# The start of a two-block transformer kernel: modulation weights become the stationary operand, the x/rms products change engine, and a fourth FFN chunk joins the tile-by-tile work

## The chip, the cores and the metric

The kernel runs on one core of one Trainium2 chip. The metric is device time in microseconds (us) of one execution. Engines are called by the short names of the profile: PE is TensorE (matmuls), PEld its weight loads, DVE is VectorE, ACT is ScalarE, POOL is GpSimd, SP issues most of the DMAs. L820 is line 820 of the kernel.

## The reference, cut to what matters

Two blocks run one after the other on x (512 tokens, width 1024). The part that the change touches is the very start of the first block: the modulation vectors and the first FFN's input.

```python
mod = (jax.nn.silu(c) @ ada_w + ada_b).reshape(b, 9, D_MODEL)          # c: 1024 values
mod_ctx = (jax.nn.silu(c_ctx) @ ada_w + ada_b).reshape(1, 9, D_MODEL)  # the same weights, a second vector
...
h = modulate(rms_norm(x, norm_pre), mod[:, 0], mod[:, 1])   # h * (1 + scale) + shift
y = (silu(h @ w_gate) * (h @ w_up)) @ w_down                # d_ff = 2816
x = x + 0.5 * mod[:, 2] * rms_norm(y, norm_post)
```

Everything after it (the context stream, the mixer, the second FFN, two attention blocks) is the same in both kernels.

## The kernel before

All of x and every hidden state lie transposed in SBUF: eight tiles k = 0..7 of 128 features by 512 tokens. A product in the precision that is wanted is made of three fp32r matmuls: each operand is split into a high part (a cast on ACT, L77 or L99) and a low part (a subtraction on DVE, L78 or L100), and high by high, high by low and low by high are added in PSUM. A weight chunk of 128 by 1024 (512 KB) is loaded by SP into `raw` (`eraw` during the start, a ring of six buffers) and split by `wchunk`.

The start (`start`, everything ahead of L1529) works as follows. SP loads x, then sixteen half chunks of `ada_w`, with FFN chunks of `f1_gu` in between. `start_squares` and `start_norm` (L1539 to L1563) make 1/rms and the eight products x/rms, called `xr`; these products run on POOL. Eight modulation chunks are made by `ada_chunk` (L230): chunk j = 4m + q gives quarter q (two of the eight feature tiles) of modulation row m, and rows 0 (shift) and 1 (scale) are needed at once. The chunks come in pairs, (q, 4+q), for q = 0..3. Each is two half chunks, each split as above, and 16 matmuls in which the stationary operand is the four columns of `c4` (two condition vectors, high and low parts) and the moving operand is 256 columns of weights (L237). That leaves a result of 4 rows by 256 columns in PSUM; ACT copies it out (L240, tile `asb`), and two small fp32 matmuls with the constant `comb` (L244) transpose it and add high and low parts; DVE adds the bias into `mod` (L247).

When pair q is there, DVE makes the scales `s1` of tiles 2q and 2q+1 (L1518), ACT makes the modulated tile `st` (L1522) and its high part `hhx` (L99), DVE its low part `hlx` (L100). Then the FFN chunks loaded so far are multiplied by these two tiles (`mm_run`, L820: 3 matmuls per tile and chunk, each 128x128 by 128x512). Three FFN chunks are worked tile by tile in this way (gate and up of f = 0, gate of f = 1), in buffers lent by tiles that are needed later (`ya`, `yc`); their sums lie in PSUM banks `y` and `pt`. The fourth (up of f = 1) is an ordinary chunk of `ffn`, multiplied by L96 in one run of 24 matmuls, and so are all that follow. PSUM has eight banks under four names; in the start x sums and norms use `pt` and `y`, modulation uses `px` and `s`.

A scheduler with priorities orders each engine's instructions; each engine then runs its own list strictly in that order. After the start, the other 28 modulation chunks are made piece by piece on DVE (`ada_sums`), five pieces per weight chunk after the first seven calls of `wchunk` in the FFN.

Of the kernel before, what the change touches and what calls it, by code (L numbers as in the profile page):

```python
# [7 lines left out]
F32 = mybir.dt.float32  # L8
F32R = mybir.dt.float32r
# [3 lines left out]
ALU = mybir.AluOpType  # L13
# [6 lines left out]
KT = D // 128  # L20
# [3 lines left out]
SLOT = 1024  # L24
# [12 lines left out]
class K:  # L37
# [135 lines left out]
    def norm_steps(self, x, y, c, G, h, s, shift, xd, run):  # L173

        r = {}

        def put():
            for k in range(KT):
                self.nc.sync.dma_start(xd[k][:, c], x[k][:, c])

        out = [lambda: r.update(p=self.rstd(y, c, run))]
        out += [lambda k=k: self.post_norm_add(x, y, c, G, r["p"], range(k, k + 2)) for k in range(0, KT, 2)]
        out += [lambda: r.update(n=self.rstd(x, c, run))]
        out += [lambda k=k: self.norm_split(x, c, h, s, shift, r["n"], range(k, k + 2)) for k in range(0, KT, 2)]
        return out + [put]
# [28 lines left out]
    def ada_setup(self):  # L214
        nc, c = self.nc, self.const
        cc = c.tile([128, KT, 2], F32, name="cc")
        nc.sync.dma_start(cc, self.I["cc"])
        sc = self.sc = c.tile([128, KT, 2], F32, name="sc")
        nc.scalar.activation(sc, cc, AF.Silu)
        self.c4 = c.tile([128, KT, 4], F32R, name="c4")  # L220
        nc.scalar.copy(self.c4[:, :, 0:2], sc)
        nc.vector.tensor_tensor(self.c4[:, :, 2:4], sc, self.c4.bitcast(F32)[:, :, 0:2], op=ALU.subtract)
        self.comb = c.tile([4, 2], F32, name="comb")
        nc.scalar.dma_start(self.comb, self.I["comb"])
        self.mod = c.tile([128, 9, KT, 2], F32, name="mod")

    def ada_chunk(self, j):

        nc = self.nc
        m, q = divmod(j, 4)  # L230
        t = self.ps("a")
        ps = t[0:4, 0:256]
        for a in range(2):
            w = self.wchunk(self.I["ada_w"][j, a])
            for i in range(2):
                for k in range(4):
                    nc.tensor.matmul(ps, self.c4[:, 4 * a + k, :], w[i][:, k * 256:(k + 1) * 256],  # L237
                                     start=(a == 0 and i == 0 and k == 0), stop=(a == 1 and i == 1 and k == 3))
        sb = self.ap.tile([4, 256], F32, name="asb", tag="asb", bufs=2)
        nc.scalar.copy(sb, ps)  # L240

        def end():
            for u in range(2):
                nc.tensor.matmul(t[:, 256 + 2 * u:258 + 2 * u], sb[:, u * 128:(u + 1) * 128], self.comb,  # L244
                                 start=True, stop=True)
            b = self.v("ada_b")[:, m * KT + 2 * q:m * KT + 2 * q + 2]
            nc.vector.tensor_tensor(self.mod[:, m, 2 * q:2 * q + 2, :],  # L247
                                    t[:, 256:260].rearrange("p (a b) -> p a b", b=2),
                                    b.unsqueeze(2).to_broadcast([128, 2, 2]), op=ALU.add)

        return end

    def ada_sums(self, j):

# [1092 lines left out]
    def run(self):  # L1347
        tc, nc, I = self.tc, self.nc, self.I
        H = (slice(0, 256), slice(256, 512))
        with ExitStack() as es:  # L1350
            self.setup(es)
            self.banks("x:pt y/m:pt y/a:px s")
            h = self.hl(es.enter_context(tc.tile_pool(name="hp", bufs=1)), T, "x")
# [6 lines left out]
            yp = rh.enter_context(tc.tile_pool(name="yp", bufs=1, side="right"))  # L1360
            ra = ExitStack()
            xa = ra.enter_context(tc.tile_pool(name="xa", bufs=1, side="right"))
            x = self.tiles(xa, T, "xa")
            with tc.tile_pool(name="st", bufs=1) as self.ap:
                with tc.high_priority(offset=AHEAD):
                    self.ada_setup()
                    first = self.start(self.ap, x, h, [(xa, "ya", 4), (xa, "ya", 4), (yp, "yc", 2)])
            self.banks("x:px s pt/m:y/a:y")
            y = [xa.tile([128, 2, T], F32, name="ya", tag="ya", bufs=4) for _ in range(4)]
            y = [t[:, j, :] for t in y for j in range(2)]  # L1370
            yc = [yp.tile([128, 4, TC], F32, name="yc", tag="yc", bufs=2) for _ in range(2)]
            yc = [t[:, j, :] for t in yc for j in range(4)]
# [29 lines left out]
            with tc.tile_pool(name="ssa", bufs=1) as sp:  # L1402
                with tc.tile_pool(name="fop", bufs=1) as fp, tc.tile_pool(name="csp", bufs=1) as gp:
# [11 lines left out]
                    f = self.fourier(fw, h, fp)  # L1415
# [11 lines left out]
            x, y = self.tiles(xb, T, "xb"), self.tiles(xb, T, "yb")  # L1427
# [34 lines left out]
            for l in range(2):  # L1462
# [4 lines left out]
                with tc.tile_pool(name="at", bufs=1) as self.at:  # L1467
                    mm = self.attention(l, h)
                    x = [mg.tile([128, 4, T], F32, name=q, tag=q) for q in ("yth", "ytl")]
                    x = [t[:, j, :] for t in x for j in range(4)]  # L1470
# [21 lines left out]
    def start(self, pool, x, h, rooms):  # L1492


        nc = self.nc
        for k in range(KT):
            nc.sync.dma_start(x[k], self.I["xT"][k])
        nc.sync.dma_start(self.tri, self.I["tri"])
        nc.sync.dma_start(self.vec, self.I["vec"])
        self.early = pool  # L1500
        self.s1 = [self.const.tile([128, KT], F32, name=f"s1{w}") for w in range(2)]
        sq = self.start_squares(pool, x)
        ends = [[self.ada_chunk(q), self.ada_chunk(4 + q)] for q in range(2)]
        self.start_norm(pool, x, sq)
        out, ws = [], []

        def chunk(i):
            p, tag, bufs = rooms[i]
            into = [p.tile([128, SLOT], F32R, name=tag, tag=tag, bufs=bufs) for _ in range(2)]
            ws.append(self.wchunk(self.I["f1_gu"][i // 2, i % 2], into=into))  # L1510
            out.append(self.ps("x"))

        for q in range(4):
            for f in ends[q]:
                f()
            ks = slice(2 * q, 2 * q + 2)
            for w in range(2):
                nc.vector.scalar_tensor_tensor(self.s1[w][:, ks], self.mod[:, 1, ks, w], 1.0, self.v("f1pre")[:, ks],  # L1518
                                               op0=ALU.add, op1=ALU.mult)
            for k in (2 * q, 2 * q + 1):  # L1520
                t = pool.tile([128, T], F32, name="st", tag="st", bufs=2)
                nc.scalar.activation(t, self.xr[k], AF.Identity, bias=self.mod[:, 0, k, 0:1], scale=self.s1[0][:, k:k + 1])  # L1522
                self.split(h[k][0], h[k][1], t)
            if q < 2:
                for i in range(2 * q, min(2 * q + 2, len(rooms))):
                    chunk(i)
                ends.append([self.ada_chunk(q + 2), self.ada_chunk(q + 6)])
            done = [range(0, 2 * q + 2) if q == 1 and i > 1 else range(2 * q, 2 * q + 2) for i in range(len(ws))]
            for w, t, kk in zip(ws, out, done):  # L1529
                self.mm_run(t, w, h, slice(0, T), kk)  # L1530
        self.early = None
        return list(zip(ws, out))
# [12 lines left out]
    def start_norm(self, pool, x, acc):  # L1545

        nc = self.nc
        ps = self.ps("m")
        for j in range(4):
            nc.tensor.matmul(ps[:, j:j + 1], acc[:, j * 128:(j + 1) * 128], self.ones[:, 0:1], start=True, stop=True)  # L1550
        v = pool.tile([128, 4], F32, name="sv")
        nc.vector.tensor_scalar(v, ps[:, 0:4], 1.0 / D, EPS, op0=ALU.mult, op1=ALU.add)
        rt = self.rsqrt(pool, v, [128, 4], "s")
        r = self.ps("m")
        for j in range(4):
            nc.tensor.matmul(r[:, j * 128:(j + 1) * 128], rt[:, j:j + 1].to_broadcast([128, 128]), self.ident,
                             start=True, stop=True)
        rs = pool.tile([128, T], F32, name="srs")
        nc.vector.tensor_copy(rs, r)
        self.xr = []  # L1560
        for k in range(KT):
            self.xr.append(pool.tile([128, T], F32, name=f"xr{k}"))
            nc.gpsimd.tensor_tensor(self.xr[k], x[k], rs, op=ALU.mult)  # L1563

    def ctx_norm(self, pool, hc):

# [109 lines left out]
def lay_out(i):  # L1676

    def fm(a):
        return np.ascontiguousarray(a.T.reshape(KT, 128, -1))

    o = {"xT": fm(i["x"][0]), "cT": fm(i["ctx"][0])}
    o["cc"] = np.ascontiguousarray(np.stack([i["c"][0].reshape(KT, 128).T, i["c_ctx"].reshape(KT, 128).T], axis=2))
    o["comb"] = np.array([[1, 0], [0, 1], [1, 0], [0, 1]], np.float32)
    items = [("ada_b", i["ada_b"][0])]
    for p, n in (("f1", "ffn1"), ("mx", "mix"), ("f2", "ffn2")):
        items += [(p + "pre", i[n + "_norm_pre"][0]), (p + "post", i[n + "_norm_post"][0])]
# [10 lines left out]
    w = i["w_in"][0]  # L1697
# [12 lines left out]
    w = i["w_in_2"]  # L1710
# [40 lines left out]
```

## Time and profile before

| | |
|---|---|
| time, median of 3 runs | 3499.43 us (3496.61 to 3499.68) |
| profiled execution: own time | 3494.87 us |
| profiled execution: span from first to last instruction | 3493.1 us |
| mean granted TensorE clock | 0.991 |
| HBM traffic over the span | 94 GB/s |

The span is what the profile describes; the time of an execution is a little longer (here 1.8 us). Busy shares are per engine over the span. A matmul's row lasts longer than the spacing to the next one, since matmuls are pipelined; rates are read from start to start. One instruction in fp32r leaves one record of PE and one of PEld; one in plain fp32 leaves two of each (the four-fold sums of L1550 and L1556, four instructions each, stand in the trace with x8).

### The profile page before, as it was taken

The page shows a single profiled execution, that of the slowest core. Times are in us where ns is not written, and L with a number is a line of the kernel's source. Part 1 is how long each engine was busy: PE and PEld are TensorE (multiplying, and loading weights), DVE is VectorE, ACT ScalarE, POOL GpSimd, SP SyncE. Part 2 cuts the span into 40 slices and gives each one's busy share as a digit, 9 for nine tenths or more (in the row PEclk, how much of TensorE's full clock was granted, in tenths as well). Part 3 has the DMA queues.
Part 4 walks back from the last instruction along what each step waited for, and adds up shares of the span by engine and source line. Part 5 has one row for each costly group of instructions (what it writes and reads, how often), then busy time and mean ns, then how long its engine had stood idle before and what let it go on. Part 6 is the DMA issues. An engine that isn't in the chain of part 4 may idle for free.

```text
span 3493.1 us, 49244 instructions
## 1 busy us (share of the span) xinstructions
PE 3428.1 (98%) x19332; PEld 2937.4 (84%) x19332; DVE 2011.8 (58%) x4119; ACT 1288.2 (37%) x2334; POOL 103.1 (3%) x147
## 2 busy tenths in 40 slices
PE   7999999999899999999999999999999999999998
PEld 5888889878888887888889898889788888898888
DVE  7466554857742338835545664556935454656545
ACT  5312212546533224424432343433434342334332
POOL 1000000002100000000100000000000100000000
PEclk9999999999899999999999999999999999999999
DMA  5344442422223334132432322233223423233231
GB/s 200 97 132 122 137 146 69 137 77 67 74 90 97 102 95 124 64 105 71 124 100 86 118 93 92 96 115 95 100 73 88 135 82 107 79 108 104 97 109 55
DMA packets 120720, 354.65 MB, mean 102 GB/s; under 512 B 17304, under 2 KB 28184, under 8 KB 120232
## 3 DMA queue, kind: packets, MB, share of 16 engines
q1 hardware_dynamic: 108976, 333.93, 29.6%
q0 software_dynamic: 7360, 12.59, 1.5%
q10 hardware_dynamic: 4152, 4.98, 0.4%
q8 instruction: 152, 2.49, 0.3%
q14 instruction: 80, 0.66, 0.1%
HBM read 320.47 MB, written 8.42 MB: 94 GB/s over the span
## 4 chain that ended last, share of the span: by engine, by line
PE 91%; DVE 5%; issue 2%; DMA 1%; ACT 1%; POOL 1%; SPq 0%; DVEq 0%; ACTq 0%; POOLq 0%
PE px L96 36%; PE s L96 17%; PE pt L96 15%; PE y L922 3%; PE s L463 2%; PE px L463 1%; PE px L794 1%; PE px L795 1%; PE pt L915 1%; PE px L798 1%; PE pt L463 1%; PE pt L820 1%; DVE wlo L78 1%; PE px L820 1%; PE s L820 1%
## 5 line engine op out<-in xcount | busy, mean ns | idle before, releaser
L78 DVE TENSOR_TENSOR wlo<-raw,whi 128x1024 fp32r<-128x1024 f32 (+4 forms) x549 | 587.0, 1075 | 614.4 <-ACT whi L77 290.0
L77 ACT CAST whi<-raw 128x1024 fp32r<-128x1024 f32 (+4 forms) x549 | 505.2, 930 | 891.2 <-PE px L96 438.1
L96 PE MATMUL px<-hlx,whi 128*128 128x512 f32 x1400 | 552.0, 394 | 0.0
L96 PE MATMUL px<-hhx,whi 128*128 128x512 f32 x1400 | 551.9, 394 | 0.0
L96 PE MATMUL px<-hhx,wlo 128*128 128x512 f32 x1400 | 362.2, 394 | 0.0
L96 PEld LDWEIGHTS px<-hlx,whi 128*128 128x128 f32 x1400 | 263.5, 188 | 53.3 <-issue 2.9
L96 PEld LDWEIGHTS px<-hhx,whi 128*128 128x128 f32 x1400 | 263.5, 188 | 51.5 <-issue 1.8
L96 PEld LDWEIGHTS px<-hhx,wlo 128*128 128x128 f32 x1400 | 260.3, 188 | 52.7 <-issue 1.5
L96 PE MATMUL pt<-hhx,whi 128*128 128x512 f32 (+1 forms) x448 | 176.5, 394 | 0.5 <-ACT hhx L159 0.5
L96 PE MATMUL pt<-hlx,whi 128*128 128x512 f32 (+1 forms) x448 | 175.3, 391 | 0.0
L96 PE MATMUL s<-hlx,whi 128*128 128x512 f32 x440 | 171.5, 390 | 0.0
L96 PE MATMUL s<-hhx,whi 128*128 128x512 f32 x440 | 171.5, 390 | 0.0
L912 ACT ACTIVATE ae<-asc,neg 128x256 f32<-128x256 f32 (+3 forms) x192 | 103.1, 537 | 72.8 <-DVE neg L998 41.6
L271 DVE SCALAR_TENSOR_TENSOR asb<-raw,sc,asb 128x256 f32<-128x256 f32 x280 | 123.1, 481 | 5.8 <-DMA raw<-ada_w 3.1
L794 PE MATMUL px<-whi,hhx 128*128 128x256 f32 (+1 forms) x416 | 114.2, 299 | 0.0
L795 PE MATMUL px<-whi,hlx 128*128 128x256 f32 (+1 forms) x416 | 112.3, 295 | 0.0
L96 PE MATMUL pt<-hhx,wlo 128*128 128x512 f32 (+1 forms) x448 | 111.1, 389 | 0.0
L96 PE MATMUL s<-hhx,wlo 128*128 128x512 f32 x440 | 109.4, 390 | 0.0
L96 PE MATMUL px<-yth,whi 128*128 128x512 f32 x256 | 100.5, 392 | 0.0
L96 PE MATMUL px<-ytl,whi 128*128 128x512 f32 x256 | 100.2, 391 | 0.0
L96 PEld LDWEIGHTS pt<-hhx,wlo 128*128 128x128 f32 (+1 forms) x448 | 83.4, 186 | 18.1
L96 PEld LDWEIGHTS pt<-hhx,whi 128*128 128x128 f32 (+1 forms) x448 | 83.6, 187 | 17.7 <-ACT hhx L159 0.6
(834 smaller groups left out, 7402.5 us busy)
## 6 DMA issues: line engine op xcount, KB each, us to landing
raw<-L_up SPq DMA_DIRECT2D x88, 512.0 KB, 3.6
raw<-f_gu SPq DMA_DIRECT2D x85, 512.0 KB, 3.6
raw<-L_gate SPq DMA_DIRECT2D x64, 512.0 KB, 3.7
raw<-ada_w SPq DMA_DIRECT2D x56, 512.0 KB, 3.7
raw<-f_dn SPq DMA_DIRECT2D x44, 512.0 KB, 3.6
raw<-L_dn SPq DMA_DIRECT2D x44, 512.0 KB, 3.6
raw<-L_br SPq DMA_DIRECT2D x32, 512.0 KB, 3.6
rr<-rx SPq DMA_DIRECT2D x160, 64.0 KB, 2.0
```

The source lines that it names most:

```text
L77: nc.scalar.copy(hi[:, s], raw[:, s])
L78: nc.vector.tensor_tensor(lo[:, s], raw[:, s], hi.bitcast(F32)[:, s], op=ALU.subtract)
L96: nc.tensor.matmul(out, a, b[:, cols], start=(i == 0), stop=(i == len(ops) - 1))
L271: nc.vector.scalar_tensor_tensor(o, x, s, o, op0=ALU.mult, op1=ALU.add)
L463: nc.tensor.matmul(t[:, cols], a[:, c], b[:, cols], start=(k == 0 and i == 0), stop=(k == KT - 1 and i == 2))
L794: nc.tensor.matmul(out, h[k][0][:, s], b, start=(k == 0), stop=False)
L795: nc.tensor.matmul(out, h[k][1][:, s], b, start=False, stop=False)
L798: nc.tensor.matmul(out, h[k][0][:, s], b, start=False, stop=(k == KT - 1))
L820: self.nc.tensor.matmul(out, a[:, c], b[:, cols], start=(k == 0 and i == 0), stop=(k == KT - 1 and i == 2), skip_group_check=True)
L912: nc.scalar.activation(e, s, AF.Exp, bias=negm, scale=-1.0, accum_out=sums[:, hcol:hcol + 1])
L915: nc.tensor.transpose(pt[:, j * 128:(j + 1) * 128], e[:, j * 128:(j + 1) * 128], self.ident)
L922: nc.tensor.matmul(y[:, ycol:ycol + 64], et[:, j * 128:(j + 1) * 128], vs[j], start=(j == 0), stop=(j == n // 128 - 1))
```

## The change

Four edits in the start. (1) `ada_chunk` no longer splits the weights: the raw fp32 chunk is the stationary operand, in blocks of 128 by 128, and the two columns of `sc` (silu of the two condition vectors, fp32) move. The result comes out as 128 features by 2, so the copy `asb`, the transposing matmuls and the constants `c4` and `comb` go, and the bias is added straight from PSUM. There are 16 such matmuls per chunk, 128 for the eight chunks. (2) The two chunks of a pair are no longer finished in a separate step. (3) The eight `xr` products move from POOL to DVE. (4) A fourth FFN chunk (up of f = 1) is worked tile by tile with the other three; it has no lent buffers and takes a `whi` and a `wlo` of the ordinary ring.

```diff
     def ada_chunk(self, j):
         t = self.ps("a")
-        ps = t[0:4, 0:256]
         for a in range(2):
-            w = self.wchunk(self.I["ada_w"][j, a])
-            for i in range(2):
-                for k in range(4):
-                    nc.tensor.matmul(ps, self.c4[:, 4 * a + k, :], w[i][:, k * 256:(k + 1) * 256],
-                                     start=(a == 0 and i == 0 and k == 0), stop=(a == 1 and i == 1 and k == 3))
-        sb = self.ap.tile([4, 256], F32, name="asb", tag="asb", bufs=2)
-        nc.scalar.copy(sb, ps)
-        def end():
-            for u in range(2):
-                nc.tensor.matmul(t[:, 256 + 2 * u:258 + 2 * u], sb[:, u * 128:(u + 1) * 128], self.comb,
-                                 start=True, stop=True)
+            w = self.early.tile([128, SLOT], F32, name="eraw", tag="eraw", bufs=6)
+            nc.sync.dma_start(w, self.I["ada_w"][j, a])
+            for k in range(4):
+                for u in range(2):
+                    nc.tensor.matmul(t[:, 2 * u:2 * u + 2], w[:, k * 256 + u * 128:k * 256 + (u + 1) * 128],
+                                     self.sc[:, 4 * a + k, :], start=(a == k == u == 0),
+                                     stop=(a == 1 and k == 3 and u == 1), skip_group_check=True)
...
-                    first = self.start(self.ap, x, h, [(xa, "ya", 4), (xa, "ya", 4), (yp, "yc", 2)])
+                    first = self.start(self.ap, x, h, [(xa, "ya", 4), (xa, "ya", 4), (yp, "yc", 2), None])
...
-        ends = [[self.ada_chunk(q), self.ada_chunk(4 + q)] for q in range(2)]
+        for q in range(2):
+            self.ada_chunk(q)
+            self.ada_chunk(4 + q)
...
-            nc.gpsimd.tensor_tensor(self.xr[k], x[k], rs, op=ALU.mult)
+            nc.vector.tensor_tensor(self.xr[k], x[k], rs, op=ALU.mult)
```

Line numbers of the changed kernel are 13 lower from the end of `ada_chunk` on: L237 is the bias add there, L233 the new matmul, L807 is `mm_run`, L1511 makes `st`.

How the order of instructions changes, first on PE at the very start. `y<-ones,ssq` are the sums of squares, `pt<-tri,rys` spreads 1/rms over the partitions, `s` and `px` are the modulation sums. Before:

```order
L1550 MATMUL y<-ones,ssq 128x1 x4
L1556 MATMUL pt<-tri,rys 128x128 x4
L237 MATMUL s<-whi,c_133 4x256 x4
L237 MATMUL s<-wlo,c_133 4x256 x4
...
L237 MATMUL px<-whi,c_133 4x256 x4
L244 MATMUL s<-comb,asb 128x2 x2
L237 MATMUL px<-wlo,c_133 4x256 x4
```

And in the changed kernel, up to the first FFN matmuls:

```order
L1540 MATMUL y<-ones,ssq 128x1 x4
L1546 MATMUL pt<-tri,rys 128x128
L233 MATMUL s<-sc,eraw 128x2 x8
L1546 MATMUL pt<-tri,rys 128x128 x3
L233 MATMUL s<-sc,eraw 128x2 x8
L233 MATMUL px<-sc,eraw 128x2 x16
L233 MATMUL s<-sc,eraw 128x2 x16
L233 MATMUL px<-sc,eraw 128x2 x16
L807 MATMUL y<-hhx_74,ya 128x512
L807 MATMUL y<-hlx_75,ya 128x512
L807 MATMUL y<-hhx_74,ya 128x512
L807 MATMUL y<-hhx_76,ya 128x512
```

The first half chunk now stands between the four matmuls that spread 1/rms, and all 64 two-column matmuls of the first two pairs stand ahead of the first FFN matmul; before, two FFN matmuls stand ahead of the last step (L244) of the second pair.

Second, PE from there to the end of the fourth pair: groups of L807 alternate with eight two-column matmuls. Between the first FFN matmul and the end of the third pair there are 24 L807 and 32 L233; between that and the end of the fourth pair 25 L807 and 32 L233; then 47 L807 in one run. The beginning of the fourth pair's stretch:

```order
L233 MATMUL px<-sc,eraw 128x2 x8
L807 MATMUL y<-hhx_74,yc 128x512
L807 MATMUL y<-hlx_75,yc 128x512
L807 MATMUL y<-hhx_82,ya 128x512
L807 MATMUL pt<-hhx_82,ya 128x512
L807 MATMUL y<-hhx_74,yc 128x512
L807 MATMUL y<-hhx_76,yc 128x512
L233 MATMUL s<-sc,eraw 128x2 x8
```

The third chunk's weights (`yc`) are first used right behind the third pair.

Third, ACT. Before, around the first `st`:

```order
L1522 ACTIVATE st<-xr_323,mod,s_149 128x512
L77 CAST whi<-eraw 128x1024
L99 CAST hhx_74<-st 128x512
L240 COPY asb<-s 4x256
L77 CAST whi<-eraw 128x1024
L1522 ACTIVATE st<-xr_325,mod,s_149 128x512
L77 CAST ya<-eraw 128x1024
L99 CAST hhx_76<-st 128x512
```

In the changed kernel:

```order
L1511 ACTIVATE st<-xr_282,mod,s_144 128x512
L1511 ACTIVATE st<-xr_284,mod,s_144 128x512
L99 CAST hhx_74<-st 128x512
L99 CAST hhx_76<-st 128x512
L1511 ACTIVATE st<-xr_286,mod,s_144 128x512
L1511 ACTIVATE st<-xr_288,mod,s_144 128x512
L77 CAST ya<-eraw 128x1024
L99 CAST hhx_78<-st 128x512
L77 CAST ya<-eraw 128x1024
L99 CAST hhx_80<-st 128x512
L1511 ACTIVATE st<-xr_290,mod,s_144 128x512
L1511 ACTIVATE st<-xr_292,mod,s_144 128x512
```

The first FFN chunk's cast (`ya<-eraw`) now stands behind the `st` of tiles 2 and 3 (286, 288), which need the second pair; the third chunk's cast (`yc<-eraw`, the next row) stands behind the `st` of tiles 4 and 5 (290, 292), which need the third pair.

## Rows read from the trace of the kernel before

**Rows 1.** Page, part 1: busy time, share of the span, instructions.

```profile
PE 3428.1 (98%) x19332; PEld 2937.4 (84%) x19332; DVE 2011.8 (58%) x4119; ACT 1288.2 (37%) x2334; POOL 103.1 (3%) x147
```

**Rows 2.** Windows: length, busy time by engine, granted clock, DMA.

```profile
15.20:28.70 13.50, 9.52 (x60) 6.40 (x60) 12.44 (x11) 5.96 (x8) 10.61 (x6) 1.00 0.77 267
28.70:42.30 13.60, 11.45 (x42) 7.37 (x43) 12.18 (x13) 8.64 (x13) 5.62 (x3) 0.50 0.66 199
42.30:62.10 19.80, 19.80 (x122) 14.50 (x120) 14.95 (x19) 14.76 (x21) 0.00 (x0) 1.00 0.58 197
72.50:160.00 87.50, 87.50 (x530) 77.94 (x529) 44.96 (x98) 27.89 (x49) 0.00 (x0) 1.00 0.25 82
```

**Rows 3.** Waits of PEld up to 72.5 us: total, times, longest.

```profile
PEld px L237 <- DVE wlo L78: 4.1, 3, 2.0
PEld s L237 <- DVE wlo L78: 3.5, 3, 2.7
```

**Rows 4.** Groups by line, 0 to 75 us: the work that the change replaces.

```profile
L78 DVE TENSOR_TENSOR wlo<-eraw,whi 128x1024 fp32r<-128x1024 f32 x16 | 25.6, 1618 | 1.8 <-ACT whi L77 1.8
L77 ACT CAST whi<-eraw 128x1024 fp32r<-128x1024 f32 x16 | 16.3, 1041 | 2.3 <-DMA eraw<-ada_w 2.3
L1563 POOL TENSOR_TENSOR xr<-xa,srs 128x512 f32<-128x512 f32 x8 | 16.2, 2060 | 17.6 <-DVE srs L1559 17.6
L100 DVE TENSOR_TENSOR hlx<-st,hhx 128x512 fp32r<-128x512 f32 x8 | 6.5, 819 | 2.1 <-ACT hhx L99 2.1
```

**Rows 5.** Timeline of PE, first modulation matmuls: start, length, engine, line, operands.

```profile
15.20 2.08 PE L1556 MATMUL pt<-tri,rys 128*128 128x128 f32 x8 [1.83 <-DVE rys L117]
16.93 1.20 PE L237 MATMUL s<-whi,c 128*4 128x256 f32 x4
18.63 0.62 PE L237 MATMUL s<-whi,c 128*4 128x256 f32 x4
```

**Rows 6.** Timeline of PE: end of the fourth FFN chunk.

```profile
72.03 0.48 PE L96 MATMUL pt<-hhx,wlo 128*128 128x512 f32 x1
```

**Rows 7.** Timeline: fp32 matmuls with one moving column, in unbroken runs.

```profile
11.50 1.78 PEld L1550 LDWEIGHTS y<-ones,ssq 128*128 128x128 f32 x8 [11.50 <-DVE ssq L1541]
632.90 0.98 PEld L135 LDWEIGHTS y<-ones,nsq 128*128 128x128 f32 x4
1339.27 2.29 PE L135 MATMUL y<-ones,nsq 128*128 128x1 f32 x20
```

**Rows 8.** Windows around two falls of the clock; columns as in rows 2.

```profile
629.40:632.80 3.40, 2.79 (x19) 2.50 (x20) 2.92 (x12) 1.67 (x4) 0.00 (x0) 1.00 0.72 197
632.80:636.20 3.40, 2.93 (x13) 2.49 (x12) 2.73 (x8) 2.09 (x4) 0.00 (x0) 0.50 0.09 34
1339.20:1342.80 3.60, 2.36 (x22) 2.27 (x21) 1.97 (x10) 0.81 (x3) 0.00 (x0) 1.00 0.47 153
1342.80:1346.20 3.40, 1.81 (x6) 1.51 (x7) 1.90 (x7) 0.80 (x2) 0.00 (x0) 0.50 0.01 2
```

**Rows 9.** The same first window, the norm sums' instructions (tile nsq) alone.

```profile
629.40:632.80 3.40, 1.68 (x12) 1.62 (x12) 1.45 (x4) 1.67 (x4) 1.00 0.72 197
```

**Rows 10.** Timeline of PE: 512-column matmuls, two about 40 us, a run at 70 us.

```profile
40.07 0.63 PE L820 MATMUL y<-hhx,ya 128*128 128x512 f32 x1
40.49 0.63 PE L820 MATMUL pt<-hlx,ya 128*128 128x512 f32 x1
...
70.08 1.75 PE L96 MATMUL pt<-hhx,wlo 128*128 128x512 f32 x7
```

**Rows 11.** Timeline: from a finished pair to the split chunk, PE, ACT and DVE.

```profile
61.60 0.58 PE L244 MATMUL px<-comb,asb 4*128 4x2 f32 x4
...
62.67 1.52 ACT L1522 ACTIVATE st<-xr,mod,s 128x512 f32<-128x512 f32 x2 [2.91 <-DVE s L1518]
...
65.13 1.05 ACT L77 CAST whi<-raw 128x1024 fp32r<-128x1024 f32 x1
...
35.32 1.21 DVE L78 TENSOR_TENSOR ya<-eraw,ya 128x1024 fp32r<-128x1024 f32 x1
```

More of the change, by code (lines that the diff above doesn't have):

```diff
@@ L219, in ada_setup @@
         nc.scalar.activation(sc, cc, AF.Silu)
[L220 to L224, printed above, removed]
         self.mod = c.tile([128, 9, KT, 2], F32, name="mod")
@@ L231, in ada_chunk @@
         t = self.ps("a")
-        ps = t[0:4, 0:256]
         for a in range(2):
-            w = self.wchunk(self.I["ada_w"][j, a])
-            for i in range(2):
-                for k in range(4):
-                    nc.tensor.matmul(ps, self.c4[:, 4 * a + k, :], w[i][:, k * 256:(k + 1) * 256],
-                                     start=(a == 0 and i == 0 and k == 0), stop=(a == 1 and i == 1 and k == 3))
-        sb = self.ap.tile([4, 256], F32, name="asb", tag="asb", bufs=2)
-        nc.scalar.copy(sb, ps)
-        def end():
-            for u in range(2):
-                nc.tensor.matmul(t[:, 256 + 2 * u:258 + 2 * u], sb[:, u * 128:(u + 1) * 128], self.comb,
-                                 start=True, stop=True)
[L246 to L251, printed above, removed]
+            w = self.early.tile([128, SLOT], F32, name="eraw", tag="eraw", bufs=6)
[5 more added lines that the diff above has]
+                                     stop=(a == 1 and k == 3 and u == 1), skip_group_check=True)
+        b = self.v("ada_b")[:, m * KT + 2 * q:m * KT + 2 * q + 2]
+        nc.vector.tensor_tensor(self.mod[:, m, 2 * q:2 * q + 2, :], t[:, :4].rearrange("p (a b) -> p a b", b=2),
+                                b.unsqueeze(2).to_broadcast([128, 2, 2]), op=ALU.add)
     def ada_sums(self, j):
@@ L1507, in chunk @@
         def chunk(i):
-            p, tag, bufs = rooms[i]
-            into = [p.tile([128, SLOT], F32R, name=tag, tag=tag, bufs=bufs) for _ in range(2)]
+            into = None
+            if rooms[i]:
+                p, tag, bufs = rooms[i]
+                into = [p.tile([128, SLOT], F32R, name=tag, tag=tag, bufs=bufs) for _ in range(2)]
             ws.append(self.wchunk(self.I["f1_gu"][i // 2, i % 2], into=into))
@@ L1513, in start @@
         for q in range(4):
-            for f in ends[q]:
-                f()
             ks = slice(2 * q, 2 * q + 2)
@@ L1526, in start @@
                     chunk(i)
-                ends.append([self.ada_chunk(q + 2), self.ada_chunk(q + 6)])
+                self.ada_chunk(q + 2)
+                self.ada_chunk(q + 6)
             done = [range(0, 2 * q + 2) if q == 1 and i > 1 else range(2 * q, 2 * q + 2) for i in range(len(ws))]
@@ L1682, in lay_out @@
     o["cc"] = np.ascontiguousarray(np.stack([i["c"][0].reshape(KT, 128).T, i["c_ctx"].reshape(KT, 128).T], axis=2))
-    o["comb"] = np.array([[1, 0], [0, 1], [1, 0], [0, 1]], np.float32)
     items = [("ada_b", i["ada_b"][0])]
```

## The prediction, made before the changed kernel ran

> **What bounds the kernel now.** I read the busy shares first: PE has work for 98% of the span and no other engine for more than 58% [rows 1]. So whatever the start does, its price is the moment at which PE comes out of it; after that PE runs without a gap (87.50 us busy of 87.50 us [rows 2]) and carries any shift to the end. Then the windows of the start. Between 15.2 and 42.3 us PE is not full (9.52 of 13.50 us, 11.45 of 13.60 us) while DVE nearly is (12.44 and 12.18 us); from 42.3 us on PE is full [rows 2]. The waits say what PE lacked: the low parts of the modulation weights, 4.1 + 3.5 us of waits of the weight loads on DVE's L78 [rows 3]. The same windows show a second loss: PE's granted clock was 0.50 from 28.7 to 42.3 us [rows 2], that is 1.2 instead of 2.4 GHz. So before, the start is bound first by DVE, which splits sixteen half chunks in 25.6 us (1.62 us each beside POOL's products, where later splits take 1.21 us [rows 4, 11]), then by PE.
>
> A point that both kernels pass is the end of the four first FFN chunks (96 matmuls of 512 columns). Before, the last of them starts at 72.03 us and the next matmul follows at about 72.4 us [rows 6, 2]. I call this M and compute it for the changed kernel; the difference is the change of the time.
>
> **What is taken away.** Sixteen splits leave DVE (25.6 us) and ACT (16.3 us), and POOL's 16.2 us become eight DVE products [rows 4]. The nearest row for one is L100, the same size, 0.82 us on average [rows 4]: 8 x 0.82 = 6.6 us. They run while PE works on the first two pairs, so I cost them at nothing; uncovered they would cost 6.6 us. The waits of rows 3 go. The fourth chunk's 24 matmuls are the same work in another place: nothing. The later modulation pieces begin one weight chunk later: nothing, DVE has room (44.96 of 87.50 us [rows 2]). SP issues the first two FFN chunks behind the second pair's loads as before, and loads wait for ring buffers that PE frees earlier than the casts need them: nothing.
>
> **What is added on PE.** The 128 modulation matmuls move only 2 columns, so each costs its weight load. One fp32 instruction leaves two records. The trace has the nearest thing, one moving column with a 128x128 fp32 stationary block, at both speeds [rows 7]: twenty records in 2.29 us, the last 0.24 us long, give (2.29 - 0.24)/19 = 0.108 us a record, 0.22 us an instruction, at full clock; eight in 1.78 us at the start of the program, when PE had been idle, give (1.78 - 0.33)/7 = 0.207 us, and four in 0.98 us at granted clock 0.50 give (0.98 - 0.33)/3 = 0.217 us. I take 0.42 us an instruction at the lower clock. Eight chunks are then 28 us at 2.4 GHz and 54 us at 1.2 GHz. A 512-column matmul costs (1.75 - 0.39)/6 = 0.23 us at the higher and 40.49 - 40.07 = 0.42 to 0.43 us at the lower clock [rows 10]; the 96 of them are 22 us or 41 us.
>
> **Which clock.** This decides, so I looked at what PE did before each fall. From 629.4 to 632.8 us PE was busy 2.79 of 3.40 us, but 1.68 us of that were one-column sums (twelve records), and the clock then stood at 0.50 [rows 8, 9]. From 1339.27 us twenty one-column records ran back to back for 2.29 us, a pause followed, and the clock was 0.50 from 1342.8 us [rows 7, 8]. Being busy with weight loads and hardly any columns did not hold the clock there. It rose only behind stretches of wide matmuls: at the start after L1556 and L237 (four L237 take 1.20 us from 16.93 us, 0.62 us from 18.63 us [rows 5]) and at 42.3 us after the L820 of rows 10. In the changed kernel one fp32 L1546 is followed by 0.42 us instructions with two columns each, 64 of them ahead of the first FFN matmul. I therefore expect 1.2 GHz from 15 us to about 47 us, and a doubtful clock where FFN and modulation matmuls alternate.
>
> The Trainium skill, in "TensorE: Matmul & The Clock Gate", section "LDWEIGHTS (loading the stationary operand)", gives a load as P/1.2 ns with P the columns, 107 ns for 128, with no word of the clock. The trace agrees at full clock (0.108 us) and differs at granted clock 0.50, where a record takes 0.217 us. By the page the eight chunks would cost 27 us at either clock, by the rows up to 54 us.
>
> **The walk.** PE starts L1546 at 15.20 us as before [rows 5] (1.78/8 x 2 = 0.44 us an instruction at this clock). One of them, 8 two-column (3.36), three (1.32), 24 two-column (10.1) bring pair 1 to 30.4 us; 32 more (13.4) bring pair 2 to 43.8 us. The first FFN cast stands on ACT behind the `st` of tiles 2 and 3, which need pair 2. From rows 11: 62.67 - 62.18 = 0.5 us from the last matmul to `st`, 1.52 us for two, 1.05 us for the cast, so 3.1 us in which PE has nothing: 46.9 us. Then 24 FFN matmuls (10.3) and 32 two-column (13.4), and 0.4 us more for the first low part (1.21 us after the cast, less two matmuls): pair 3 at 71.0 us. Again 3.1 us, since the third chunk's cast waits behind `st` of tiles 4 and 5: 74.1 us. Then 25 FFN matmuls (10.8), 32 two-column (13.4), 0.4: pair 4 at 98.7 us. The last 47 run without a break; their `st` and split are covered by the first 23. With some 5 us at 1.2 GHz (12 matmuls) and 35 at 0.23 us they take 13.1 us: M = 111.8 us, 39.4 us later than before.
>
> That is the upper bound. For the lower one the clock rises within the first mixed stretch, some 4 us behind 46.9 us, and comes back after the next gap: three quarters of pair 3's stretch at the higher clock (18 x 0.20 + 24 x 0.20 = 8.4 us less), pair 4's whole (25 x 0.20 + 32 x 0.20 = 11.4 us less), the last 47 whole (2.4 us less). M = 89.6 us, 17.2 us later. Nothing in the rows says when such a mixture lifts the clock; I take a little over the middle, since PE falls idle for 3.1 us between the two stretches and the clock may fall again: 30 us. The profiled execution took 3494.87 us and would take 3525; it lay 4.6 us under the median of the runs, so the forecast is 3499.4 + 30 = **3529 us**.
>
> **The rivals.** *The clock rises about when it did before (18.5 us) and stays.* For it: PE is busy without a pause from 15.2 us. Against it: rows 8 and 9. The walk with 0.22 and 0.23 us: pair 1 at 25.0, pair 2 at 32.0, FFN from 35.1, pair 3 at 48.4, FFN from 51.5, pair 4 at 64.6, M = 75.4 us: +3 us, 3502. Even so PE does more than it did (28 us of modulation matmuls) and waits twice for 3.1 us, so nothing is gained.
>
> *A weight load takes the same time at either clock* (0.107 us a record), and only the wide matmuls slow down. Against it: the 0.98 us row of rows 7. Pairs at 23.8 and 30.6, FFN from 33.7, pair 3 at 51.2, FFN from 54.3, pair 4 at 72.3, M = 85.4 us: +13, 3512. This is the page's rule above.
>
> *Faster: a two-column fp32 instruction leaves one record, not two,* and so costs 0.11 us at a clock that is full from 18.5 us. It decides from the price alone: the first rival's walk less 128 x 0.11 = 14 us gives M = 61.4, 11 us earlier, 3488. For it: fp32r instructions leave one record. Against it: the four instructions of L1550 left eight.
>
> **The numbers.** A change within 0.2% (7 us) can hardly be told from none here. Forecast with its bounds (3516 to 3540): 0.83. Clock as before, within 0.2%: 0.10. Clock-blind loads, slower: 0.04. One record, faster: 0.03. So slower 0.87, same 0.10, faster 0.03. The range reaches below the likeliest case's own to take in part of the second rival, and 2 us above it for a clock that stays down: 3507 to 3542.
>
> **What would show it.** Right: granted clock 0.50 through the stretch of L233, records 0.21 us apart; no PE wait on L78 for modulation, but two gaps of about 3 us ahead of the first `ya` and the first `yc` matmul, ended by ACT's L77; DVE and ACT far from full; M near 102 us; behind M the same rows as before, shifted. Wrong: L233 records 0.11 us apart before 40 us, or M under 80 us. The forecast also fails if PE, once late, finds gaps to close behind M; I see none in the full 87.50 us [rows 2].

## The result and the profile after

The changed kernel takes 3527.13 us (median of 5 runs, 3525.88 to 3531.32) against 3499.43 us (5 runs, 3494.39 to 3500.56) for the kernel before on the same chip: ratio 1.0086, 95% interval 1.0072 to 1.0100. It is slower by 28 us, where 29.6 us were forecast. Where a comparison below had a disturbed run (3761.55 us of one experiment, 6808.29 us of the kernel before), that run is left out.

The profiled execution of the changed kernel took 3531.32 us (span 3529.5 us). Its page, part 1, shows where the work went, to be read beside [rows 1]:

```profile
PE 3464.4 (98%) x19428; PEld 2978.3 (84%) x19428; DVE 1988.0 (56%) x4110; ACT 1269.7 (36%) x2309; POOL 86.9 (2%) x139
```

DVE, ACT and POOL all have less to do than before, by 23.8, 18.5 and 16.2 us. PE has 36.3 us more, and PE is what ends the kernel. The stretch to look at is the start. PE's timeline there, first the modulation of pairs 1 and 2 (start, length, engine, line, operands, count; behind a row the idle time before it and what ended that):

```profile
15.29 0.80 PE L1546 MATMUL pt<-tri,rys 128*128 128x128 f32 x2 [1.84 <-DVE rys L117]
15.88 3.41 PE L233 MATMUL s<-sc,eraw 128*128 128x2 f32 x16
19.15 1.63 PE L1546 MATMUL pt<-tri,rys 128*128 128x128 f32 x6
20.57 3.41 PE L233 MATMUL s<-sc,eraw 128*128 128x2 f32 x16
23.85 6.96 PE L233 MATMUL px<-sc,eraw 128*128 128x2 f32 x32
30.67 6.96 PE L233 MATMUL s<-sc,eraw 128*128 128x2 f32 x32
37.50 6.97 PE L233 MATMUL px<-sc,eraw 128*128 128x2 f32 x32
47.46 0.79 PE L807 MATMUL y<-hhx,ya 128*128 128x512 f32 x1 [2.99 <-ACT ya L77]
...
59.98 0.63 PE L807 MATMUL pt<-hlx,ya 128*128 128x512 f32 x1
60.41 0.63 PE L807 MATMUL pt<-hhx,ya 128*128 128x512 f32 x1
...
68.51 1.88 PE L233 MATMUL px<-sc,eraw 128*128 128x2 f32 x16
73.39 0.80 PE L807 MATMUL y<-hhx,yc 128*128 128x512 f32 x1 [2.99 <-ACT yc L77]
...
88.74 1.84 PE L233 MATMUL px<-sc,eraw 128*128 128x2 f32 x16
90.44 0.48 PE L807 MATMUL pt<-hhx,wlo 128*128 128x512 f32 x1
...
101.44 0.50 PE L135 MATMUL y<-ones,nsq 128*128 128x1 f32 x4
```

Rates are read from start to start. From 23.85 to 30.67 us are 32 records of L233, two for each instruction: 6.82 / 32 = 0.213 us a record, 0.427 us an instruction. From 88.74 to 90.44 us sixteen records take 1.70 / 16 = 0.106 us each, half of that. Two 512-column matmuls stand 0.43 us apart at 60 us, as [rows 10] have it at the lower clock. The same instruction at two speeds, and both kinds slow at once: the first 53 us of the stretch ran at 1.2 GHz. The four first FFN chunks end at 101.44 us, where before it was 72.4 us [rows 6]: M came 29.0 us later.

The two gaps of 2.99 us stand ahead of the first `ya` and the first `yc` matmul. What ends them is in ACT's timeline:

```profile
44.96 1.52 ACT L1511 ACTIVATE st<-xr,mod,s 128x512 f32<-128x512 f32 x2 [9.49 <-DVE s L1507]
46.38 1.03 ACT L77 CAST ya<-eraw 128x1024 fp32r<-128x1024 f32 x1
...
70.88 1.52 ACT L1511 ACTIVATE st<-xr,mod,s 128x512 f32<-128x512 f32 x2 [21.48 <-DVE s L1507]
72.31 1.03 ACT L77 CAST yc<-eraw 128x1024 fp32r<-128x1024 f32 x1
```

ACT had been idle for 9.49 and 21.48 us. The FFN chunks were there in that time (in e4_poolcast below, POOL casts the same ones from 31.38 and 50.73 us on), but ACT's list has an `st` ahead of the cast, and that `st` needs the next pair. The waits of PE and PEld between the first L233 and M name the same two places and no split of modulation weights, which were waits of the weight loads before [rows 3] (total, times, longest):

```profile
PE y L807 <- ACT ya L77: 3.0, 1, 3.0
PE y L807 <- ACT yc L77: 3.0, 1, 3.0
PEld y L807 <- DVE ya L78: 0.8, 1, 0.8
```

The windows, columns as in [rows 2], hold a trap:

```profile
25.00:30.00 5.00, 5.00 (x25) 5.00 (x25) 2.20 (x4) 0.00 (x0) 0.00 (x0) 1.00 0.67 191
70.00:75.00 5.00, 2.01 (x8) 1.63 (x8) 2.03 (x5) 4.12 (x6) 0.00 (x0) 0.70 0.73 241
75.00:80.00 5.00, 5.00 (x22) 4.61 (x21) 1.93 (x3) 0.32 (x1) 0.00 (x0) 0.50 0.44 180
85.00:90.00 5.00, 5.00 (x39) 4.61 (x37) 0.00 (x0) 0.00 (x0) 0.00 (x0) 1.00 0.00 0
110.00:200.00 90.00, 90.00 (x554) 80.97 (x553) 42.50 (x83) 28.46 (x48) 0.00 (x0) 1.00 0.30 91
```

The granted clock reads 1.00 from 25 to 30 us, while the records there are 0.213 us apart, and 25 of them fit into the 5 us; from 85 to 90 us, also at 1.00, it is 39 with wide matmuls among them. So the column does not show the clock of the first 68 us, and the spacing of like records does. Only from the first change that it shows (a fall in the gap behind 70.4 us) do column and spacing agree: 0.50 from 75 to 80 us, and a rise before 85 us, which the spacing puts at about 82 us. The last row is the rest of the kernel: PE full, as before.

### The profile page after: what moved, and what is told of

Its sections match the earlier page's. It is cut to its first block, busy times and chain, and to the rows that moved or that the text cites. A ratio compares the mean times of both kernels' runs of the same rounds, so it can differ in the third digit from the quotient of the medians.

```text
span 3529.5 us, 49363 instructions
## 1 busy us (share of the span) xinstructions
PE 3464.4 (98%) x19428; PEld 2978.3 (84%) x19428; DVE 1988.0 (56%) x4110; ACT 1269.7 (36%) x2309; POOL 86.9 (2%) x139
## 4 chain that ended last, share of the span: by engine, by line
PE 91%; DVE 4%; issue 1%; DMA 1%; ACT 1%; POOL 0%; SPq 0%; DVEq 0%; ACTq 0%; POOLq 0%
PE px L96 36%; PE s L96 16%; PE pt L96 15%; PE y L909 3%; PE s L450 1%; PE px L450 1%; PE px L781 1%; PE pt L902 1%; PE px L782 1%; PE px L785 1%; PE pt L450 1%; PE pt L807 1%; PE px L807 1%; PE s L807 1%; PE s L233 1%
## 5 line engine op out<-in xcount | busy, mean ns | idle before, releaser
L78 DVE TENSOR_TENSOR wlo<-raw,whi 128x1024 fp32r<-128x1024 f32 (+4 forms) x548 | 585.5, 1074 | 616.0 <-ACT whi L77 288.3
L77 ACT CAST whi<-raw 128x1024 fp32r<-128x1024 f32 (+4 forms) x548 | 504.3, 930 | 901.5 <-PE px L96 451.8
L96 PE MATMUL px<-ytl,whi 128*128 128x512 f32 x256 | 101.4, 396 | 0.0
L96 PEld LDWEIGHTS s<-hhx,whi 128*128 128x128 f32 x440 | 82.6, 188 | 16.9
```

Source lines behind the costliest of these rows:

```text
L77: nc.scalar.copy(hi[:, s], raw[:, s])
L78: nc.vector.tensor_tensor(lo[:, s], raw[:, s], hi.bitcast(F32)[:, s], op=ALU.subtract)
L96: nc.tensor.matmul(out, a, b[:, cols], start=(i == 0), stop=(i == len(ops) - 1))
```

## Experiments

M, the end of the four FFN chunks, is read in every trace. Where matmuls of the fifth chunk already stand ahead of it, 0.23 us for each is taken off. M comes from the one profiled execution of each kernel. Times are medians beside those of the kernel before in the same session (3498.33 us, 21 runs, for e1 to e4; 3498.82 us, 32 runs, for the others); e2 and e4 have 4 runs, the other experiments 10 or 11.

| kernel | M us | M against 72.4 | time us | against before | ratio, 95% |
|---|---|---|---|---|---|
| after | 101.4 | +29.0 | 3527.13 | +27.7 | 1.0086 [1.0072, 1.0100] |
| e1_wide | 69.6 | -2.8 | 3497.93 | -0.4 | 1.0000 [0.9991, 1.0009] |
| e2_warm | 95.0 | +22.6 | 3518.93 | +20.6 | 1.0062 [1.0049, 1.0076] |
| e3_oldmod | 70.9, less 11 matmuls: 68.4 | -4.0 | 3494.36 | -4.0 | 0.9991 [0.9982, 1.0000] |
| e4_poolcast | 103.0 | +30.6 | 3529.62 | +31.3 | 1.0093 [1.0079, 1.0107] |
| e5_hybrid | 68.9, less 15 matmuls: 65.5 | -6.9 | 3490.82 | -8.0 | 0.9977 [0.9968, 0.9987] |
| e6_dveonly | 71.4 | -1.0 | 3495.03 | -3.8 | 0.9990 [0.9981, 0.9999] |
| e7_fouronly | 75.3, less 12 matmuls: 72.5 | +0.1 | 3497.86 | -1.0 | 0.9996 [0.9987, 1.0005] |
| e9_wideg | 69.6 | -2.8 | 3496.70 | -2.1 | 0.9996 [0.9987, 1.0005] |

The shift of M gives the change of the time to within 3 us in all of them, about what runs of one kernel differ by. So M is the right thing to argue about.

Where an expectation names a theory by a letter, A is the prediction's own: the two-column fp32 matmuls cost their weight loads, these take twice as long at 1.2 GHz, and the clock neither comes up nor holds while they run. The rivals: B, the loads are slow in this place whatever moves; C, only a PE that comes cold into the stretch is to blame; D, the loss is that of the other edits, (3) and (4).

**e1_wide: the same weight loads with 128 columns moving.** The two columns are repeated 64 times (tile `sw`), and two of the 128 results are used; the arithmetic that counts is the same. The 1/rms matmuls stand ahead of the modulation.

```diff
-                    nc.tensor.matmul(t[:, 2 * u:2 * u + 2], w[:, k * 256 + u * 128:k * 256 + (u + 1) * 128],
-                                     self.sc[:, 4 * a + k, :], start=(a == k == u == 0),
+                    nc.tensor.matmul(t[:, 128 * u:128 * u + 128], w[:, k * 256 + u * 128:k * 256 + (u + 1) * 128],
+                                     self.sw[:, 4 * a + k, :], start=(a == k == u == 0),
```

> The changed kernel, but the modulation matmuls move 128 columns (the two condition columns repeated 64 times) instead of 2; 1/rms is emitted ahead of the modulation chunks. Same number of weight loads, 64 times the columns. Theory A (the moving width sets the clock): loads cost what they did, the clock is up soon after 20 us, records 0.11 us apart, the first FFN chunks end near 69 us, time about 3496 us. Theory B (the loads themselves take 0.21 us a record in this place, whatever moves): records stay 0.21 us apart, 3525 us or more.

PE's timeline of it:

```profile
16.00 2.08 PE L1550 MATMUL pt<-tri,rys 128*128 128x128 f32 x8 [1.84 <-DVE rys L117]
17.87 4.51 PE L237 MATMUL s<-sw,eraw 128*128 128x128 f32 x32
22.23 3.74 PE L237 MATMUL px<-sw,eraw 128*128 128x128 f32 x32
25.80 3.74 PE L237 MATMUL s<-sw,eraw 128*128 128x128 f32 x32
29.37 3.74 PE L237 MATMUL px<-sw,eraw 128*128 128x128 f32 x32
```

Sixty-four times the columns, and half the time: 3.57 us from start to start for 32 records, 0.112 us each, where the changed kernel has 0.213. Inside the first group the rate changes (4.36 us from start to start), that is, the clock came up within the first few microseconds and stayed. The first two pairs take 15.2 us in one run, instead of 27.2 us (the three L1546 instructions that stood among them not counted), so no order is involved there. The scheduler also put the `ya` casts ahead of the next `st` in this kernel, and PE has no wait between 17.87 and 60 us. The 31.9 us less to M than in the changed kernel add up: the modulation matmuls take 29.1 us instead of 47.3 us (18.2 less), the 96 FFN matmuls 22.6 us instead of 30.8 us (8.2 less), the two gaps are gone (6.0 less), and the 1/rms matmuls start 0.7 us later but take 0.1 us less. This run takes the slow clock and the two gaps away together; the sum, and not the run by itself, says what each was worth.

**e2_warm: PE kept busy ahead of the stretch.** Forty-two matmuls on constants, 128 columns each, fill PE's idle time around the sums of squares; their results are not used.

```diff
+        self.wt = self.ps("x")
+        for i in range(34):
+            nc.tensor.matmul(self.wt[:, 0:128], self.ones, self.ones, start=True, stop=True)
         sq = self.start_squares(pool, x)
...
+        for i in range(8):
+            nc.tensor.matmul(self.wt[:, 0:128], self.ones, self.ones, start=True, stop=True)
```

> The changed kernel with 42 idle 128-column fp32 matmuls on constants ahead of and between the norm's matmuls, so that PE's clock is up when the two-column matmuls begin; their results are not used. Theory A (two columns don't hold the clock up): the records start 0.11 us apart and fall back to 0.21 us within some 5 us; 3522 to 3528 us. Theory C (only the cold start was to blame, a clock once up stays up): 0.11 us through the first two pairs, the FFN chunks end near 75 us, about 3502 us.

Its PE timeline, then its windows, in which the granted clock has a first change early and can be read:

```profile
15.08 1.84 PE L233 MATMUL s<-sc,eraw 128*128 128x2 f32 x16
16.78 0.69 PE L1551 MATMUL pt<-tri,rys 128*128 128x128 f32 x4
17.31 2.99 PE L233 MATMUL s<-sc,eraw 128*128 128x2 f32 x16
20.16 6.96 PE L233 MATMUL px<-sc,eraw 128*128 128x2 f32 x32
```

```profile
15.00:18.00 3.00, 3.00 (x29) 3.00 (x28) 0.49 (x1) 0.00 (x0) 0.00 (x0) 0.96 1.05 404
18.00:21.00 3.00, 3.00 (x15) 3.00 (x16) 1.56 (x4) 0.00 (x0) 0.00 (x0) 0.50 0.56 178
```

The stretch begins at full clock, 0.106 us a record, and about 3 us later the clock falls to 0.50 with PE busy for 3.00 of 3.00 us in both windows. So the low clock is not a leftover of the idle start: a busy PE lost the clock while it ran two-column matmuls. Pair 2 ends 3.7 us earlier than in the changed kernel, and the clock came back earlier in the mixed stretch too (at 58 us instead of 68 us), which makes 6.4 us in M. The time lies 3 us below the range that was expected, since the earlier return of the clock was not in it; the rows don't tell why it came back earlier.

**e3_oldmod: the kernel before with edits (3) and (4) alone.**

```diff
-                    first = self.start(self.ap, x, h, [(xa, "ya", 4), (xa, "ya", 4), (yp, "yc", 2)])
+                    first = self.start(self.ap, x, h, [(xa, "ya", 4), (xa, "ya", 4), (yp, "yc", 2), None])
...
-            nc.gpsimd.tensor_tensor(self.xr[k], x[k], rs, op=ALU.mult)
+            nc.vector.tensor_tensor(self.xr[k], x[k], rs, op=ALU.mult)
```

> The kernel before with the other two edits alone: x/rms on DVE, the fourth FFN chunk tile by tile; the modulation as before (split weights moving, four columns stationary). Theory A: these edits cost nothing, 3496 to 3503 us: eight products of 0.8 us come onto DVE, and the splits, no longer beside POOL, fall from 1.6 to about 1.2 us each. Theory D (the loss is DVE's and the fourth chunk's): 3510 us or more.

These two edits do not cost time; if anything they gain 4.0 us (the interval ends at 1.0000). Its groups by line up to 75 us (count, then busy time and mean ns of one) show what changed on DVE:

```profile
L78 DVE TENSOR_TENSOR wlo<-eraw,whi 128x1024 fp32r<-128x1024 f32 x17 | 20.1, 1219 | 0.0
L1565 DVE TENSOR_TENSOR xr<-xa,srs 128x512 f32<-128x512 f32 x8 | 5.3, 684 | 0.0
```

The products cost DVE 5.3 us, and the splits, 1618 ns each beside POOL's products [rows 4], take 1219 ns without them.

**e6_dveonly and e7_fouronly: the two edits apart.** The first has the second pair of lines of the diff above, the other the first pair.

> The kernel before with one edit: the x/rms products on DVE. Theory A: DVE takes 6 us more but its first splits run in 1.2 instead of 2.2 us; no loss, and perhaps the 4 us that the two edits together gained: 3494 to 3499 us. Theory D (DVE was the bound, so work moved onto it costs): 3503 us or more.

> The kernel before with one edit: the fourth FFN chunk tile by tile. It fills PE's waits of the start with 24 more matmuls that may run there, so if the two edits' gain of 4 us is its doing, 3494 to 3496 us; if it only moves work inside a full PE, 3498 us.

With the products on DVE alone the 16 splits take 19.0 us instead of 25.6 us (first line); with the fourth chunk alone they stay slow (second line):

```profile
L78 DVE TENSOR_TENSOR wlo<-eraw,whi 128x1024 fp32r<-128x1024 f32 x16 | 19.0, 1218 | 0.5 <-ACT whi L77 0.5
L78 DVE TENSOR_TENSOR wlo<-eraw,whi 128x1024 fp32r<-128x1024 f32 x17 | 26.8, 1596 | 1.6 <-ACT whi L77 1.6
```

DVE saves 6.6 us for 5.3 us of new work; the time is 3.8 us less, at the edge of what can be measured (interval 0.9981 to 0.9999), and M in its trace is only 1.0 us earlier. The fourth chunk alone changes nothing that can be measured (0.9987 to 1.0005), and the splits still take 1596 ns on average. So what e3_oldmod gains is most likely the products' doing; at this size that is not shown.

**e4_poolcast: the changed kernel without the casts on ACT's list.** The casts of the first FFN chunks go to POOL, so that no `st` stands ahead of them.

```diff
-            nc.scalar.copy(hi[:, s], raw[:, s])
+            (nc.gpsimd.tensor_copy if self.early is not None else nc.scalar.copy)(hi[:, s], raw[:, s])
```

> The changed kernel with the casts of the first four FFN chunks on POOL instead of ACT, so that they don't queue behind the modulated tiles that need the next pair. Theory A prices the two gaps ahead of the first ya and yc matmul at 3 us each; the low parts on DVE still wait for the next pair, so each gap should shrink to 1 or 2 us: 3522 to 3526 us. If the gaps are covered by something else: 3527 us.

PE's timeline at the two gaps and later:

```profile
46.39 1.22 PE L807 MATMUL y<-hhx,ya 128*128 128x512 f32 x2 [0.60 <-DVE ya L78]
...
72.16 0.80 PE L807 MATMUL y<-hhx,ya 128*128 128x512 f32 x1 [1.51 <-ACT hhx L99]
...
81.28 3.41 PE L233 MATMUL s<-sc,eraw 128*128 128x2 f32 x16
...
86.41 0.63 PE L807 MATMUL pt<-hhx,wlo 128*128 128x512 f32 x1
86.83 0.63 PE L807 MATMUL pt<-hhx,whi 128*128 128x512 f32 x1
...
87.67 1.84 PE L233 MATMUL px<-sc,eraw 128*128 128x2 f32 x16
```

A miss. The gaps shrank from 2.99 to 0.60 and 1.51 us, 3.9 us in all, and yet M is 1.5 us later. In the changed kernel the clock was up from about 68.4 us to the gap, and again from about 82 us; here the slow rows go on without a break until about 87 us (two wide matmuls still 0.42 us apart at 86.41 us). The sums over the stretch say the same: 50.0 us for the 128 modulation matmuls instead of 47.3 us, 33.3 us for the 96 FFN matmuls instead of 30.8 us, 5.2 us given back. Why the clock did not come up at 68 us in this run, the rows don't show. So this run does not price the gaps; that they cost 6.0 us stays a reading of the changed kernel's trace.

**e9_wideg: e1_wide with the copies that build `sw` on POOL.**

```diff
-            nc.vector.tensor_copy(self.sw[:, k, :].rearrange("p (r c) -> p r c", c=2),
+            nc.gpsimd.tensor_copy(self.sw[:, k, :].rearrange("p (r c) -> p r c", c=2),
```

> The version with 128 moving columns, the copies of the condition columns made on POOL instead of DVE, where they delayed the sums of squares (the norm's first matmul began at 12.30 instead of 11.59 us). PE has no gap after that point, so the 0.7 us should come out of the time: 3497 us; within the spread of the runs.

It can't be told from e1_wide (M 69.64 and 69.55 us), nor from the kernel before. The 0.7 us did not come: the norm's first matmul begins at 12.12 us, 0.2 us earlier than in e1_wide, and M is no earlier.

**e5_hybrid: wide stationary weights for pairs 1 and 2, the split way for pairs 3 and 4,** with edits (3) and (4). `ada_wide` is the function of e1_wide, `ada_chunk` that of the kernel before.

```diff
+        ends = [[], []]
         for q in range(2):
-            self.ada_chunk(q)
-            self.ada_chunk(4 + q)
+            self.ada_wide(q)
+            self.ada_wide(4 + q)
...
-                self.ada_chunk(q + 2)
-                self.ada_chunk(q + 6)
+                ends.append([self.ada_chunk(q + 2), self.ada_chunk(q + 6)])
```

> Pairs 1 and 2 of the modulation with stationary fp32 weights and 128 moving columns, pairs 3 and 4 as in the kernel before (split weights moving), with the other two edits kept. Theory A: with the clock up, PE's work is 14.3 us for four wide chunks, 9.2 us for four old ones and 22 us of FFN matmuls from 17.1 us on, the first FFN chunks end at 63 to 66 us, time 3490 to 3493 us, under both kernels. If DVE's and ACT's splits of the last two pairs hold PE up again: 3494 to 3498 us.

PE's timeline of it:

```profile
15.72 2.07 PE L1583 MATMUL pt<-tri,rys 128*128 128x128 f32 x8 [1.83 <-DVE rys L117]
17.58 4.63 PE L242 MATMUL s<-sw,eraw 128*128 128x128 f32 x32
22.05 3.74 PE L242 MATMUL px<-sw,eraw 128*128 128x128 f32 x32
...
34.16 0.62 PE L259 MATMUL s<-whi,c 128*4 128x256 f32 x4
34.62 0.39 PE L842 MATMUL pt<-hhx,ya 128*128 128x512 f32 x1
...
68.94 0.50 PE L135 MATMUL y<-ones,nsq 128*128 128x1 f32 x4
```

In the first two pairs DVE is relieved while PE would wait for splits, in the last two PE is relieved (four 256-column matmuls from 34.16 us on take 0.46 us from start to start) while DVE has time. PE waits nowhere from 17.58 to 68.94 us, and behind the first group, which takes 4.47 us from start to start, its records stand as at full clock. M as the trace has it is later than was expected, since 15 matmuls of the fifth chunk stand ahead of it; without these it is 65.5 us. The hybrid is faster than both kernels: 0.23% under the one before (interval 0.9968 to 0.9987), and about 1% under the changed one (their ratios to the kernel before, 0.9977 and 1.0086, come from different sessions). Whether it beats e3_oldmod is not settled, the intervals overlap.

## Why the prediction was right

**The price of an instruction.** Predicted 0.42 us at 1.2 GHz and 0.22 us at 2.4 GHz, from one-column sums [rows 7]. Measured 0.427 and 0.212 us. The 128 of them took 47.3 us, between the bounds of 28 and 54 us. The rival of one record an instruction fell: 128 instructions left 256 records.

**The clock.** That it would neither rise nor hold under two-column matmuls was read from what PE did ahead of two falls [rows 8, 9]. The runs show it for this stretch: the same loads with 128 columns come to full clock (e1_wide), and a PE that begins the stretch at full clock loses it (e2_warm). The rival of a clock that rises as before (M 75.4 us) fell with that.

The rival of loads that do not know the clock (M 85.4 us) fell too: 0.213 us a record in a stretch of nothing but L233, 0.106 us in another. The Trainium skill ("TensorE: Matmul & The Clock Gate", section "LDWEIGHTS (loading the stationary operand)") gives P/1.2 ns for P columns, 107 ns for 128, and names no clock; the trace agrees at full clock alone.

**The walk.** Predicted: pair 1 at 30.4, pair 2 at 43.8, FFN from 46.9, pair 3 at 71.0, FFN from 74.1 us. Measured: 30.8, 44.5, 47.5, 70.4, 73.4 us. The two gaps are 2.99 us each (3.1 predicted) and ended by ACT's L77, as the order of `st` and cast had it. Pair 3 ended 0.6 us before the walk's time although pair 2 had ended 0.7 us behind it, because its last sixteen records ran at full clock, 1.7 us that the walk did not have. From there the walk left the clock open, pair 4 at 98.7 us if it stayed low; it ended at 90.6 us, the clock having risen for good at about 82 us. The lower bound had the clock rise 4 us behind the first FFN matmul; it rose 21 us behind it, and again about 9 us behind the second gap. The choice of "a little over the middle" gave M near 102 us: measured 101.44 us. That part was an estimate between bounds, not a derivation, and e2_warm and e4_poolcast show how much such a moment can move (M 95 to 103 us). The range was earned; that the forecast came within 2 us was luck.

**What was costed at nothing.** The fourth chunk is worth nothing, as said (e7_fouronly, in the kernel before). The products on DVE were set at nothing, covered by PE; in the changed kernel no wait of PE names them, and they end at 32.8 us, while PE is in the second pair. The splits that they would speed up are gone there. But the reasoning missed that next to splits moving them looks like a gain in itself: 3.8 us in e6_dveonly, at the edge of what can be measured. The prediction had the number in hand, 1.62 us a split beside POOL against 1.21 us later [rows 4, 11], and used it only to describe the bound.

**What would show it.** Most of the signs came as told: the records 0.21 us apart, no PE wait on L78 for modulation, the two gaps, DVE and ACT far from full, M. One was wrong in form: the granted clock was to read 0.50 through the stretch of L233, and it read 1.00. Read alone, that column would have called the right mechanism wrong.

**Behind M** the kernel runs as before, shifted. The two profiled executions differ by 36.5 us, 7.4 us more than M does, while the medians differ by 27.7 us. Part of the 7 us can be placed: PE waits longer for one DMA far behind the start, and the clock falls there, which it did not do before (for each kernel the row of PE and a window around it, before first; columns of the windows as in [rows 2]):

```profile
2641.79 0.30 PE L892 MATMUL s<-pile 128*128 128x128 f32 x1 [0.89 <-DMA pile<-ph]
2630.00:2660.00 30.00, 29.07 (x158) 23.76 (x156) 21.29 (x53) 16.14 (x40) 7.15 (x14) 1.00 0.59 161
2676.24 0.34 PE L879 MATMUL s<-pile 128*128 128x128 f32 x1 [2.63 <-DMA pile<-ph]
2662.00:2692.00 30.00, 27.33 (x136) 22.23 (x135) 17.81 (x45) 12.98 (x31) 6.12 (x12) 0.94 0.61 158
```

The wait is 1.7 us longer, and a mean granted clock of 0.94 over 30 us costs some 1.8 us (an estimate from these rows). The traces of e2_warm and e4_poolcast, whose starts are late too, show no such fall, and the profiled execution of after was the slowest of its five. So I put the 7 us down to the spread of runs and not to the change, which is argued and not shown.

## What to carry to other kernels

Before making wide weights the stationary operand of a matmul with a few columns, price it by its weight loads at the lower clock, not by its columns: here 128 instructions that come to 28 us at the full clock's price cost 47 us, and the wide matmuls among them were slow too (30.8 us instead of the 22.6 us of e1_wide). Splits on DVE that are the bound were better relieved in part: in the stretch where PE waits for them, and with 128 moving columns, with which PE kept its clock (e5_hybrid). When an in-order engine has both early and late work, look at what stands ahead of the early piece on its list, for its being idle (9.5 and 21.5 us here) does not mean that it could do it.

## What the runs showed of the hardware that was not expected

- **The granted clock of the profile can read full before its first recorded change.** In the changed kernel it is 1.00 up to 68 us while like records stand 0.213 us apart, and 0.106 us later in the trace. The same can be seen before, with hindsight: four L237 in 1.20 us beside 0.62 us in one window of 1.00 [rows 2, 5]. The mean clock hides it, 0.991 in both kernels. The Trainium skill ("TensorE: Matmul & The Clock Gate", section "Seeing it yourself") warns that the recorded clock events are not to be trusted one by one. In this trace the changes that are recorded agree with the rows; it is the stretch ahead of the first of them that misleads. The spacing of like records is the check.
- **More columns were faster.** With 128 columns instead of 2 the same 32 records took 3.57 us instead of 6.82 us.
- **POOL beside DVE.** Beside eight POOL products of 2.06 us the 16 DVE splits took 25.6 us, without them 19.0 us (e6_dveonly): the difference is more than the 5.3 us that the products cost on DVE itself. The Trainium skill ("GPSIMD Engine Reference", section "8. Key points") says that GpSimd shares its SBUF interfaces with VectorE and contends with instructions that have two SBUF inputs, as the splits have. The runs agree in that the slowing goes when POOL's work goes.
